# Two transformer blocks on one core: modulation rows among the natural projections, attention's left-over work in slots, overflow loops last, SyncE loads

## The chip, the core and the metric

The kernel is one program on one core of a Trainium2 chip. The metric is the device time of one execution in microseconds (us). A core has five instruction streams: TensorE (PE; its weight loads are listed as PEld), VectorE (DVE), ScalarE (ACT), GpSimd (POOL) and SyncE (SP). SP, POOL and ACT also start DMA transfers. Each stream runs its instructions in order and waits on semaphores for the others.

## What is computed

A sequence of 1024 latent rows of width 1024 (and 256 context rows) goes through two blocks. Block one modulates its normed rows by `silu(c) @ w_ada + b_ada`, runs differential attention (4 heads, two softmax maps a head) and gated linear attention (GLA), and then a mixture of 32 experts, two for each row. Block two has a gated linear recurrence, multi-head latent attention, and a mixture of 64 experts, two for each row. All is float32.

```python
shift1, scale1, gate1, shift2, scale2, gate2 = split(silu(c) @ w_ada + b_ada, 6)
h   = rms_norm(x) * (1 + scale1) + shift1
a_l = rms_norm(softmax(q0 k0) v - lam * softmax(q1 k1) v) * (1 - lambda_init)
g_l = rms_norm(gla(q, k, v, gates)) * silu(r)
x   = x + gate1 * (concat(a_l, g_l) @ w_out)
x   = x + gate2 * moe(rms_norm(x) * (1 + scale2) + shift2)     # 32 experts, top 2
x   = x + rnn_and_mla(rms_norm(x))
x   = x + moe_2(rms_norm(x))                                   # 64 experts, top 2
```

## The kernel before

The program goes through stages, one behind the other. Times are those of the profiled execution, from the start of the span:

1. **Front** (0 to about 100). The modulation that the first projection needs is made, the rows are normed, modulated and split into a high and a low half (`hTh`, `hTl`); every projection is three matmuls, high by high, low by high and high by low.
2. **Natural projections** (to about 412, loop at L395): `plan` lists slabs of 256 columns of `w_in`; `nat` does one tile of 128 rows for a slab (24 matmuls of 256 columns), and the result `po` goes to DRAM (`gqk`, `gv`, `sg`, `vs`). Between the tiles `gla_units` (L465) runs GLA step by step; it reads its values as one tile `g_v` for each of two halves `p`.
3. **Heads** (to about 541): `heads` makes the transposed queries and keys with their rotary embedding and writes them to `qs` and `ks`. Between its blocks it takes two steps of `ada_rows` (L236), which makes the four remaining parts of the modulation (gate1, shift2, scale2, gate2) as rows: a 512 KB load `wada`, two DVE multiply-adds over 128x512 into `aacc` (L250, L252), and after every fourth step a matmul `ad` that sums the partitions (L257), an addition (L258) and a store to `rows`. There are 32 steps.
4. **Attention** (to about 870): `phase1b` (L760) walks `da_units` (L662): 4 query blocks by 4 heads by 2 maps. The scores `s` of a map are copied out with their maximum (`da_e`, L697), exponentiated on ACT, and weighted on POOL or DVE. What is left (`da_turn` L722 turns the weights, `da_out` L731 multiplies by the values, norms the head with a POOL power at L745 and writes it) sits in one list `late` that keeps three items waiting. Between the maps another generator takes a step: `out_weights` (L961) first, then `mix_units` (L777) of the query block before.
5. **Mix and routing** (`phase1c`, L1002, to about 950), which also issues the first expert loads.
6. **Experts of block one** (`moe1`, L1227, to about 1515): 24 rounds of 8 MB of weights (`m_w`, loaded by SP), a gather `m_x`, and a scatter-add `x1d<-m_y` on POOL.
7. **Block two**: norms, recurrence, gates, latent attention, output (to about 2655).
8. **Experts of block two** (`moe2`, L1943, to the end): 32 pairs of experts, for each pair 6 MB of weights (`n_w`, `n_d`), a gather `n_x` and a scatter-add `out<-n_y`. SP loads the first pairs; from pair 3 on POOL issues the loads (`load(p + 3, ..., nc.gpsimd)`), behind the scatter of the pair.

`overflow` (L1085) is a loop over experts that got more rows than their capacity, with a trip count read from memory (`nc.values_load`, then `tc.For_i`, L1125 and L1126). Its count is zero here. All five streams go through the loop's branch, and POOL waits there for every transfer that it has started. It stands in round 15 of `moe1` (L1312) and behind pair 25 of `moe2` (L2037).

The order inside a stream is set by a scheduling layer that records the stages and interleaves them; the order rows below show the outcome.

Of the kernel before, what the change touches and what calls it, by code (L numbers as in the profile page):

```python
# [13 lines left out]
ALU = mybir.AluOpType  # L14
# [8 lines left out]
NA = 10  # L23
# [44 lines left out]
class Kern:  # L68
# [110 lines left out]
    def phase1a(self, keep, dram):  # L179
# [12 lines left out]
        with tc.tile_pool(name="p1a", bufs=1) as pool, tc.tile_pool(name="p1a_ps", bufs=1, space=PSUM) as psum:  # L192
# [43 lines left out]
            def ada_rows(ap):  # L236


                todo = [(s, h) for s in range(4, 12) for h in range(4)]
                ws = [ada_load(ap, *x, 3) for x in todo[0:3]]  # L240
                for n, (s, h) in enumerate(todo):
                    if h == 0:
                        acc = self.t(ap, [P, 512], tag="aacc", bufs=2)
                        row = self.t(ap, [1, 2, 512], tag="arow", bufs=2)
                        nc.sync.dma_start(row[:, 0, :], a["b_ada"][:, ts(s, 512)])
                    w = ws.pop(0)
                    for i in range(2):
                        c = c16[:, 2 * h + i:2 * h + i + 1]
                        if h + i == 0:
                            nc.vector.tensor_scalar(acc, w[:, 0, :], c, None, op0=ALU.mult)  # L250
                        else:
                            nc.vector.scalar_tensor_tensor(acc, w[:, i, :], c, acc, op0=ALU.mult, op1=ALU.add)  # L252
                    if n + 3 < len(todo):
                        ws.append(ada_load(ap, *todo[n + 3], 3))
                    if h == 3:
                        pb = self.t(psum, [P, 512], tag="ad", bufs=2)
                        self.mm(pb[0:1, :], self.mats[:, 6, 0:1], acc, True, True)  # L257
                        nc.vector.tensor_tensor(row[:, 1, :], row[:, 0, :], pb[0:1, :], op=ALU.add)  # L258
                        nc.sync.dma_start(self.rows[s // 2 - 2:s // 2 - 1, ts(s % 2, 512)], row[:, 1, :])
                    yield  # L260

# [125 lines left out]
            gla = self.gla_units(gp, psum)  # L387
            ready = {0: 2, 1: 5}
            done, waiting = 0, next(gla)
            w = slab(*first, raw)  # L390
            for i, (cols, n, tiles, fin) in enumerate(plan):
# [3 lines left out]
                for t in tiles:  # L395
                    nat(w, n, t, fin)
                    if waiting is None or i >= ready[waiting]:
                        waiting = next(gla, 2)
                        if waiting == 2:
                            ready[2] = 99  # L400
                w = nxt
            while waiting != 2:
                waiting = next(gla, 2)
            gla_cm.__exit__(None, None, None)
# [5 lines left out]
            with tc.tile_pool(name="p1a_r", bufs=1, reuse_waits="tile") as back:  # L410
                rope = self.t(back, [P, 2, S], tag="rope")
                nc.gpsimd.dma_start(rope, a["k_rope"])
                rows = ada_rows(back)
# [41 lines left out]
                for _ in rows:  # L455
                    pass
# [8 lines left out]
    def gla_units(self, pool, psum):  # L465
# [18 lines left out]
        for p in range(2):  # L484
            yield p
            v = self.t(pool, [P, NA, 256], tag="g_v")
            nc.sync.dma_start(v, self.gv[:, ts(p, 256)].rearrange("(t p) n -> p t n", p=P))
# [47 lines left out]
            def stage_b(t, qk, eb, ei, er):  # L535
# [4 lines left out]
                nc.vector.tensor_tensor(four(kt), k4, four(er if t < 2 else ei), op=ALU.mult)  # L540
                kv = [self.t(psum, [P, 256], tag="g", bufs=3) for c in range(2)]
                for h in range(2):
                    for c in range(2):
                        self.mm(kv[c][:, ts(h, P)], kt[64 * c:64 * c + 64, ts(h, P)], v[64 * c:64 * c + 64, t, ts(h, P)],
                                True, True)
# [45 lines left out]
            def stage_d(t, sm):  # L591
                s0 = P * (t - 2)
                po = self.t(psum, [P, 2, P], tag="g", bufs=3)
                for h in range(2):
                    for d in range(2):
                        self.mm(po[:, h, :], sm[:, d, h, :], v[:, t, ts(h, P)], d == 0, False)
# [48 lines left out]
    def da_load(self, qb, h):  # L645
# [12 lines left out]
        v = self.t(self.daq, [P, NA, P], tag="da_v", bufs=2)  # L658
        nc.sync.dma_start(v, self.vs[:, ts(h, P)].rearrange("(t p) n -> p t n", p=P))
        self.da_in[qb, h] = qd, kst, v  # L660

    def da_units(self, pool, psum, cp):  # L662
# [14 lines left out]
        late = []  # L677
        kb = [(0, 512), (512, 512), (1024, 256)]
        for qb in range(4):
            for h in range(4):  # L680
                qd, kst, v = self.da_in.pop((qb, h))
                if qb < 3 or h < 3:
                    self.da_load(*((qb, h + 1) if h < 3 else (qb + 1, 0)))
                groups = [self.t(pool, [P, 4, 256], tag="da_a", bufs=4) for g in range(3)]
                es0 = self.t(pool, [P, 2], tag="da_es", bufs=3)
                for j in range(2):
# [4 lines left out]
                    for m in range(2):  # L691
# [9 lines left out]
                        es.append(e)  # L701

# [19 lines left out]
    def da_turn(self, psum, e, groups, j):  # L722
        nc = self.nc
        for g in range(3):
            nk = 4 if g < 2 else 2
            pt = self.t(psum, [P, 4, P], tag="tp", bufs=3)
# [1374 lines left out]
```

## Time and profile before

| | |
|---|---|
| median of 3 runs | 3222.18 us (3221.11 to 3223.78) |
| profiled execution | 3225.12 us, of which its span is 3223.3 us |
| busy in the span | PE 90%, DVE 42%, ACT 31%, POOL 15% |
| mean granted TensorE clock | 0.958 of full speed |
| moved by DMA | 705.72 MB, mean 219 GB/s |

Busy shares are means over stages with different limits, so the profile is read stage by stage: in the table of windows below, an engine near the length of its window is what bounds that window. The last two columns are the share of time in which the 16 DMA engines were busy, and the bytes that they moved. The groups of rows further below are numbered for the text that follows them.

### The profile page before, as it was taken

The page shows a single profiled execution, that of the slowest core. Times are in us where ns is not written, and L with a number is a line of the kernel's source. Part 1 is how long each engine was busy: PE and PEld are TensorE (multiplying, and loading weights), DVE is VectorE, ACT ScalarE, POOL GpSimd, SP SyncE. Part 2 cuts the span into 40 slices and gives each one's busy share as a digit, 9 for nine tenths or more (in the row PEclk, how much of TensorE's full clock was granted, in tenths as well). Part 3 has the DMA queues.
Part 4 walks back from the last instruction along what each step waited for, and adds up shares of the span by engine and source line. Part 5 has one row for each costly group of instructions (what it writes and reads, how often), then busy time and mean ns, then how long its engine had stood idle before and what let it go on. Part 6 is the DMA issues. An engine that isn't in the chain of part 4 may idle for free.

```text
span 3223.3 us, 45952 instructions
## 1 busy us (share of the span) xinstructions
PE 2895.1 (90%) x17841; PEld 1945.5 (60%) x17841; DVE 1365.4 (42%) x3217; ACT 985.8 (31%) x2006; POOL 482.3 (15%) x520
## 2 busy tenths in 40 slices
PE   6999997799969999897899999999998988777758
PEld 4989875677743333232777788878876973323223
DVE  4244377867651111111567512478875361111101
ACT  4355311555410000000656413256664111100001
POOL 2000011222210101000100000111001103333332
PEclk8999998899989999999899999999999999999989
DMA  6223278676478999995422443322246469999988
GB/s 220 92 83 102 82 249 233 172 182 171 136 298 332 391 403 400 345 393 205 156 65 82 137 161 113 108 74 66 56 121 209 149 233 364 407 378 365 394 330 299
DMA packets 282109, 705.72 MB, mean 219 GB/s; under 512 B 33784, under 2 KB 168080, under 8 KB 233120
## 3 DMA queue, kind: packets, MB, share of 16 engines
q1 hardware_dynamic: 230880, 462.06, 42.4%
q0 software_dynamic: 44320, 222.85, 18.9%
q10 hardware_dynamic: 6688, 17.83, 1.5%
q8 instruction: 142, 2.33, 0.3%
q14 instruction: 79, 0.65, 0.1%
HBM read 616.08 MB, written 99.11 MB: 222 GB/s over the span
## 4 chain that ended last, share of the span: by engine, by line
PE 24%; DMA 17%; DVE 6%; ACT 2%; issue 2%; POOL 1%; SPq 0%; POOLq 0%; DVEq 0%; ACTq 0%
PE mm L88 19%; DMA n_d<-exp_w 12%; DMA n_w<-exp_w 2%; PE s L88 1%; PE o L88 1%; PE gt L88 1%; DMA oTs<-od 1%; POOL m_rs L101 1%; DMA ws<-w_mla_o 1%; DVE wl L1340 1%; PE tp L1868 1%; PE lg L88 0%; DVE m_al L1872 0%; ACT wh L1339 0%; DVE m_e L1847 0%
## 5 line engine op out<-in xcount | busy, mean ns | idle before, releaser
L88 PE MATMUL mm<-m_w,m_xTf 128*32 128x512 f32 x3072 | 343.4, 599 | 10.0 <-issue 10.0
L88 PE MATMUL mm<-n_w,n_xTf 128*64 128x512 f32 x1024 | 268.2, 637 | 83.9 <-DMA n_w<-exp_w 62.7
L88 PEld LDWEIGHTS mm<-n_w,n_xTf 128*64 128x64 f32 x1024 | 91.1, 147 | 254.9 <-issue 254.3
L88 PEld LDWEIGHTS mm<-m_w,m_xTf 128*32 128x32 f32 x3072 | 96.0, 111 | 221.2 <-issue 215.3
L88 PE MATMUL mm<-uTh,wh 128*128 128x512 f32 x512 | 205.4, 401 | 0.0
L88 PE MATMUL mm<-uTh,wl 128*128 128x512 f32 x512 | 203.4, 397 | 0.0
L88 PE MATMUL mm<-uTl,wh 128*128 128x512 f32 x512 | 202.5, 396 | 0.0
L88 PE MATMUL mm<-wh,hTh 128*128 128x256 f32 (+1 forms) x608 | 178.1, 293 | 1.9 <-ACT wh L288 1.9
L88 PE MATMUL mm<-wh,hTl 128*128 128x256 f32 (+1 forms) x608 | 176.0, 289 | 1.7 <-DVE hTl L351 1.7
L88 PE MATMUL mm<-wl,hTh 128*128 128x256 f32 (+1 forms) x608 | 175.0, 288 | 0.5 <-DVE wl L289 0.5
L88 PE MATMUL mm<-m_w,m_hTf 128*32 128x512 f32 x1536 | 171.1, 592 | 0.9 <-DVE m_hTf L1071 0.9
L1340 DVE TENSOR_TENSOR wl<-ws,wh 128x512 fp32r<-128x512 f32 x128 | 90.0, 717 | 167.7 <-ACT wh L1339 167.4
L1071 ACT COPY m_xTf<-tp 128x512 f32<-128x512 f32 x24 | 14.1, 586 | 426.5 <-PE tp L1065 392.3
L2023 DVE TENSOR_TENSOR n_h<-n_h,mm 128x256 f32<-128x256 f32 x32 | 13.5, 421 | 306.4 <-ACT n_h L2022 306.4
L88 PE MATMUL s<-da_k,da_q 128*128 128x512 f32 (+1 forms) x384 | 117.4, 414 | 14.9 <-DVE da_e L697 14.5
L88 PE MATMUL mm<-n_d,n_hTf 128*64 128x512 f32 x512 | 117.0, 598 | 14.1 <-DVE n_hTf L1071 14.0
L1287 DVE SCALAR_TENSOR_TENSOR m_y<-mm,o_w,gt 128x512 f32<-128x512 f32 x48 | 36.0, 751 | 213.7 <-PE mm L88 210.8
L88 PEld LDWEIGHTS mm<-wh,hTh 128*128 128x128 f32 x608 | 115.9, 191 | 9.8 <-issue 5.6
L88 PEld LDWEIGHTS mm<-m_w,m_hTf 128*32 128x32 f32 x1536 | 50.4, 110 | 115.9 <-issue 115.2
L88 PEld LDWEIGHTS mm<-wh,hTl 128*128 128x128 f32 x608 | 116.0, 191 | 4.1 <-DVE hTl L351 2.7
L88 PEld LDWEIGHTS mm<-wl,hTh 128*128 128x128 f32 x608 | 116.1, 191 | 2.9 <-issue 1.3
L1339 ACT CAST wh<-ws 128x512 fp32r<-128x512 f32 x128 | 77.6, 619 | 128.7 <-PE mm L88 51.2
(542 smaller groups left out, 6533.2 us busy)
## 6 DMA issues: line engine op xcount, KB each, us to landing
n_w<-exp_w POOLq DMA_DIRECT2D x112, 1024.0 KB, 17.0
m_w<-expert_w_gate SPq DMA_DIRECT2D x64, 1024.0 KB, 10.0
m_w<-expert_w_up SPq DMA_DIRECT2D x64, 1024.0 KB, 10.5
m_w<-expert_w_down SPq DMA_DIRECT2D x64, 1024.0 KB, 13.5
n_d<-exp_w POOLq DMA_DIRECT2D x58, 1024.0 KB, 16.8
wada<-w_ada SPq DMA_DIRECT2D x48, 512.0 KB, 4.8
da_k<-ks SPq DMA_DIRECT2D x64, 320.0 KB, 6.3
n_w<-exp_w SPq DMA_DIRECT2D x12, 1024.0 KB, 8.6
```

The costliest lines, as they stand in the source:

```text
L88: self.nc.tensor.matmul(out, l, r, start=start, stop=stop)
L101: nc.gpsimd.tensor_tensor(out, m, self.neghalf[:, 0:w], op=ALU.pow)
L1071: (nc.scalar.copy if g else nc.vector.tensor_copy)(xf[:, r, :], pt)
L1287: nc.vector.scalar_tensor_tensor(y[:, ts(c, 512)], py[c], rt["w"][:, r:r + 1], gt2[:, ts(c, 512)], op0=ALU.mult, op1=ALU.mult)
L1339: nc.scalar.copy(wh[:, r, :], st)
L1340: nc.vector.tensor_tensor(wl[:, r, :], st, wh[:, r, :].bitcast(F32), op=ALU.subtract)
L1868: nc.tensor.transpose(pt[:, i, :], e[:, ts(g0 + i, P)], self.ident)
L2023: nc.vector.tensor_tensor(h, h, ph[:, 1, :], op=ALU.mult)
```

## The change

It has seven parts.

- **Rows.** `ada_rows` works in 128 steps: a 128 KB load `wrow`, one DVE multiply-add over 128x256. There are 16 matmuls `ad` of 256 columns, each done six steps after its sum is complete. Two steps stand behind each tile of the natural projections from the second slab on.
- **GLA values.** Instead of one `g_v` tile for each half, each step loads its own 128x256 tile, once for the states and once for the output: 36 loads of 128 KB in place of 2 of 1280 KB.
- **Attention.** Each head yields four times, and the left-over work of the head before stands in four slots: turn, turn, product with the values, sum of squares; the norm follows one slot later. `phase1b` takes a step of the other generator in three of the four. The value load `da_v` moves to the start of its head.
- **Mix.** `mix_units` yields once more in each half; `phase1c` issues its 8 first expert loads one at a time.
- **Loop of `moe1`** behind the last round. **Loop of `moe2`** behind the last pair.
- **Loads of `moe2`** are all issued by SP.

```diff
...
+                todo = [(s, k) for s in range(8, 24) for k in range(8)]
+                def load(s, k):
+                    w = self.t(ap, [P, 256], tag="wrow", bufs=3)
+                    nc.sync.dma_start(w, wa[:, k, ts(s, 256)])
...
+                def finish(s, acc, row):
+                    pb = self.t(psum, [P, 512], tag="ad", bufs=2)
+                    self.mm(pb[0:1, 0:256], self.mats[:, 6, 0:1], acc, True, True)
+                    nc.vector.tensor_tensor(row, row, pb[0:1, 0:256], op=ALU.add)
+                    nc.sync.dma_start(self.rows[s // 4 - 2:s // 4 - 1, ts(s % 4, 256)], row)
...
+                ws, late = [load(*x) for x in todo[0:2]], None
+                for n, (s, k) in enumerate(todo):
+                    w, c = ws.pop(0), c16[:, k:k + 1]
+                    if k == 0:
+                        acc = self.t(ap, [P, 256], tag="aacc", bufs=2)
+                        row = self.t(ap, [1, 256], tag="arow", bufs=2)
+                        nc.sync.dma_start(row, a["b_ada"][:, ts(s, 256)])
+                        nc.vector.tensor_scalar(acc, w, c, None, op0=ALU.mult)
+                    else:
+                        nc.vector.scalar_tensor_tensor(acc, w, c, acc, op0=ALU.mult, op1=ALU.add)
+                    if n + 2 < len(todo):
+                        ws.append(load(*todo[n + 2]))
+                    if k == 5 and late:
+                        finish(*late)
+                    if k == 7:
+                        late = s, acc, row
                     yield
+                yield
+                yield
+                finish(*late)
...
                     nat(w, n, t, fin)
+                    if i:
+                        next(rows, None)
+                        next(rows, None)
...
-                            if c0 >= 256:
-                                next(rows, None)
-                                next(rows, None)
...
-            v = self.t(pool, [P, NA, 256], tag="g_v")
-            nc.sync.dma_start(v, self.gv[:, ts(p, 256)].rearrange("(t p) n -> p t n", p=P))
+            def values(t, tag):
+                v = self.t(pool, [P, 256], tag=tag, bufs=2)
+                nc.sync.dma_start(v, self.gv[ts(t, P), ts(p, 256)])
...
+                v = values(t, "g_v1")
...
-        v = self.t(self.daq, [P, NA, P], tag="da_v", bufs=2)
-        nc.sync.dma_start(v, self.vs[:, ts(h, P)].rearrange("(t p) n -> p t n", p=P))
-        self.da_in[qb, h] = qd, kst, v
+        self.da_in[qb, h] = qd, kst
...
+        behind = [[], [], [], []]
...
+        def slot(i):
+            while behind[i]:
+                f, x = behind[i].pop(0)
+                f(*x)
...
-                    late.append((self.da_turn, (psum, es[0], groups, j)))
-                    if j == 1:
-                        late.append((self.da_out, (pool, psum, cp, h, qb, v, groups, es0)))
-                    while len(late) > 3:
-                        f, x = late.pop(0)
-                        f(*x)
-                    yield qb
-        for f, x in late:
-            f(*x)
...
+                    mine.append((pool, psum, es[0], groups, j))
+                    slot(2 * j + 1)
+                    yield qb, 2 * j + 1
+                state = {}
+                behind[0].append((self.da_turn, mine[0]))
+                behind[1].append((self.da_turn, mine[1]))
+                behind[2].append((self.da_out, (pool, psum, v, groups, state)))
+                behind[3].append((self.da_ssq, (pool, psum, es0, state)))
+                behind[3].append((behind[0].append, ((self.da_norm, (psum, cp, h, qb, state)),)))
+        for i in (0, 1, 2, 3, 0):
+            slot(i)
+            yield qb, -1
...
+    def da_ssq(self, pool, psum, es0, state):
...
+    def da_norm(self, psum, cp, h, qb, state):
...
-            for i, qb in enumerate(self.da_units(pool, psum, cp)):
-                if qb != at and i % 8 >= 2:
+            for i, (qb, slot) in enumerate(self.da_units(pool, psum, cp)):
+                if qb != at and i % 16 >= 4:
                     for _ in other:
                         pass
                     other, at = self.mix_units(cp, psum, lg, qb - 1, 1, 3), qb
-                if i:
+                if i and slot != 2:
                     next(other, None)
...
+                    if k == 3:
+                        yield
...
-                if i < 4:
-                    self.moe1_load()
+                if i < 8:
                     self.moe1_load()
...
-                if r == 15:
-                    self.overflow(pool, psum, "m_", rt, self.h2d, self.x1d, wg.rearrange("e d h -> (e d) h"),
-                                  wu.rearrange("e d h -> (e d) h"), wd.rearrange("e h d -> (e h) d"), E, HID, self.cap1, gt2)
             down(ROUNDS - 1, self.turn_cols(pool, psum, h, 4, "m_hT", False))
+            self.overflow(pool, psum, "m_", rt, self.h2d, self.x1d, wg.rearrange("e d h -> (e d) h"),
+                          wu.rearrange("e d h -> (e d) h"), wd.rearrange("e h d -> (e h) d"), E, HID, self.cap1, gt2)
...
-                        eng.dma_start(w[i][:, j, k, :], m[es[i]].rearrange("(p k) n -> p k n", k=8)[:, k, :])
+                        nc.sync.dma_start(w[i][:, j, k, :], m[es[i]].rearrange("(p k) n -> p k n", k=8)[:, k, :])
...
-                    if p == 25:
-                        self.overflow(pool, psum, "n_", rt, self.h4d, self.x3d, wg.rearrange("e d h -> (e d) h"),
-                                      wu.rearrange("e d h -> (e d) h"), wd.rearrange("e h d -> (e h) d"), E, HID, cap)
                     if p + 3 < E // 2:
-                        load(p + 3, 2 if p + 4 == E // 2 else 1, nc.gpsimd)
+                        load(p + 3, 2 if p + 4 == E // 2 else 1)
+                self.overflow(pool, psum, "n_", rt, self.h4d, self.x3d, wg.rearrange("e d h -> (e d) h"),
+                              wu.rearrange("e d h -> (e d) h"), wd.rearrange("e h d -> (e h) d"), E, HID, cap)
...
```

Three places in the order of the program. First, PE at the end of `heads` and the first scores of attention (`mm` are the projections, `ad` sums a modulation row, `s` are the scores). Before:

```order
L88 MATMUL mm_5443<-hTl_109,wh_5033 128x512
L88 MATMUL ad_5363<-aacc_5308,mats_75 1x512
L88 MATMUL mm_5443<-hTh_108,wl_5034 128x512
...
L88 MATMUL mm_5443<-hTh_108,wl_5034 128x512
L88 MATMUL ad_5483<-aacc_5434,mats_75 1x512
L88 MATMUL s_5537<-da_k_5228,da_q_5227 128x512 x2
```

The changed kernel:

```order
L88 MATMUL mm_5829<-hTl_109,wh_5499 128x512
L88 MATMUL mm_5829<-hTh_108,wl_5500 128x512
L88 MATMUL s_5912<-da_k_5648,da_q_5647 128x512 x2
L88 MATMUL s_5916<-da_k_5648,da_q_5647 128x512 x2
L88 MATMUL s_5920<-da_k_5648,da_q_5647 128x256 x2
```

The last `ad` stood between the last projection and the first scores; now the scores follow the projections directly, and the 16 `ad` matmuls stand among the natural projections.

Second, SP in the second half of the natural projections of the changed kernel, where before only stores of `po` (`vs`, `sg`), GLA's transfers and the slab loads `wst` stood:

```order
L501 DMA g_v_825_3967<-gv_64 128x256
L289 DMA wst_5105<-w_in 128x4x256
L518 DMA g_qk_4030<-gqk_63 128x256
L376 DMA vs_62<-po_3931 128x256
L251 DMA rows_67<-arow_3386 1x256
L244 DMA wrow_4117<-w_ada 128x256
L244 DMA wrow_4175<-w_ada 128x256
L376 DMA vs_62<-po_4021 128x256
L244 DMA wrow_4178<-w_ada 128x256
L259 DMA arow_4111<-b_ada 1x256
L501 DMA g_v_843_4053<-gv_64 128x256
```

SP's queue now holds 128 `wrow` loads and 36 `g_v` loads between stores that wait for their `po`.

Third, POOL and SP around the two loops (the rows of L1125, L1126, L1168 and L1169 are the loop; `m_w`, `n_w` and `n_d` are weights). POOL in `moe2` before:

```order
L1081 DMA out<-n_y_25261,o_tok_21276 1024x1024
L1967 DMA n_w_4304_23582<-exp_w_2 128x2048
L1125 TENSOR_LOAD v_ni_25292
L1126 COMPARE_AND_BRANCH
L1126 ISA
...
L1967 DMA n_w_4304_23582<-exp_w_2 128x2048
L1970 DMA n_d_4306_23584<-exp_w_2 128x2048
```

POOL in `moe2` of the changed kernel:

```order
L1124 DMA out<-n_y_25894,o_tok_21656 1024x1024
L1124 DMA out<-n_y_25948,o_tok_21656 1024x1024
L1124 DMA out<-n_y_25989,o_tok_21656 1024x1024
L1168 TENSOR_LOAD v_ni_26020
L1169 COMPARE_AND_BRANCH
L1169 ISA
```

SP at the end of `moe1` of the changed kernel, where `norm_g` is the first load of block two:

```order
L1268 DMA m_w_2538_12867<-expert_w_down 128x2048
L1168 TENSOR_LOAD v_ni_13066
L1168 ISA x2
L1169 COMPARE_AND_BRANCH
...
L1543 DMA g_2667_13448<-norm_g 128x1024
L1379 DMA wzs_2670_13452<-w_in 128x4x288
```

The loop of `moe2` stood between two weight loads of POOL and now stands behind the last scatter, with no weight load left on POOL. The loop of `moe1` stands behind the last weight load and ahead of block two's first loads.

## Rows read from the trace of the kernel before

**Rows 1.** The page, busy time of the engines.
```profile
PE 2895.1 (90%) x17841; PEld 1945.5 (60%) x17841; DVE 1365.4 (42%) x3217; ACT 985.8 (31%) x2006; POOL 482.3 (15%) x520
```

**Rows 2.** Windows: natural, heads, its end, attention (two), moe1 (two), moe2's stop.
```profile
core 0: us, PE busy (x) PEld busy (x) DVE busy (x) ACT busy (x) POOL busy (x), PEclk, DMA share, GB/s
100.00:412.00 312.00, 311.93 (x2450) 279.90 (x2449) 122.88 (x343) 151.34 (x476) 11.73 (x17) 1.00 0.32 96
412.00:530.00 118.00, 107.80 (x472) 81.29 (x470) 95.17 (x149) 14.81 (x23) 21.01 (x15) 0.96 0.79 251
530.00:541.00 11.00, 2.05 (x3) 0.35 (x4) 7.50 (x15) 1.24 (x2) 1.26 (x1) 0.55 0.73 219
541.00:641.00 100.00, 77.12 (x330) 61.54 (x331) 84.04 (x218) 52.81 (x81) 23.26 (x9) 0.81 0.71 181
641.00:870.00 229.00, 223.30 (x1199) 181.54 (x1199) 156.63 (x463) 121.10 (x204) 54.50 (x32) 0.99 0.66 167
1000.00:1300.00 300.00, 300.00 (x2692) 100.13 (x2688) 45.33 (x65) 15.39 (x26) 34.13 (x26) 1.00 1.01 397
...
3100.00:3112.00 12.00, 5.63 (x29) 2.69 (x29) 2.20 (x4) 1.66 (x3) 2.66 (x5) 0.98 1.02 399
3112.00:3136.00 24.00, 2.76 (x12) 1.74 (x12) 0.69 (x1) 0.59 (x1) 3.68 (x4) 0.50 0.48 185
3136.00:3160.00 24.00, 22.64 (x102) 8.22 (x102) 3.83 (x7) 2.04 (x4) 9.26 (x14) 0.94 0.81 295
```

**Rows 3.** Timeline of POOL around moe1's loop (start, duration, engine, line, idle before).
```profile
1282.92 1.59 POOL L1081 DMA_INDIRECT x1d<-m_y,o_tok  x1 [19.50 <-DVE m_y L1287]
...
1305.56 1.58 POOL L1081 DMA_INDIRECT x1d<-m_y,o_tok  x1 [19.69 <-DVE m_y L1287]
...
1315.93 1.03 POOL L1075 DMA_INDIRECT m_x<-h2d,o_tok  x1 [7.42 <-PEq L1126]
1342.73 1.62 POOL L1081 DMA_INDIRECT x1d<-m_y,o_tok  x1 [25.77 <-DMA m_w<-expert_w_gate]
```

**Rows 4.** Timeline of PE and SP at moe1's loop.
```profile
1305.78 1.10 SPq L1225 DMA_DIRECT2D m_w<-expert_w_gate  x1
...
1325.29 0.33 SPq L1225 DMA_DIRECT2D m_w<-expert_w_up  x1
...
1325.67 4.79 PE L88 MATMUL mm<-m_w,m_xTf 128*32 128x512 f32 x24 [10.02 <-issue]
```

**Rows 5.** Timeline at the end of moe1: last scatter, then SP's next load.
```profile
1516.40 1.56 POOL L1081 DMA_INDIRECT x1d<-m_y,o_tok  x1 [14.87 <-DVE m_y L1287]
1522.85 0.33 SPq L1500 DMA_DIRECT2D g<-norm_g  x1
```

**Rows 6.** Windows: DMA share at the end of moe1's loads.
```profile
1490.00:1500.00 10.00, 10.00 (x100) 3.01 (x96) 1.50 (x2) 0.00 (x0) 0.03 (x1) 1.00 0.01 2
```

**Rows 7.** Timeline of POOL and PE at moe2's loop.
```profile
3115.72 0.58 POOL L1967 DMA_DIRECT2D n_w<-exp_w  x1 [0.43 <-issue]
3135.61 0.55 POOL L1967 DMA_DIRECT2D n_w<-exp_w  x1 [19.30 <-DVE n_xTf L1071]
...
3134.87 9.03 PE L88 MATMUL mm<-n_w,n_xTf 128*64 128x512 f32 x32 [21.24 <-issue]
```

**Rows 8.** DMA queues (packets, MB, share): moe1 1000:1300, two rows; then moe2 2800:3100.
```profile
q1 hardware_dynamic: 15053, 109.60, 88.8%
q0 software_dynamic: 3744, 9.09, 11.5%
...
q0 software_dynamic: 19412, 114.91, 99.8%
```

**Rows 9.** Groups by line, 412:541: DVE sums and the PE matmul behind them.
```profile
L252 DVE SCALAR_TENSOR_TENSOR aacc<-wada,c,aacc 128x512 f32<-128x512 f32 x56 | 49.8, 890 | 2.0 <-DMA wada<-w_ada 1.6
L88 PE MATMUL ad<-aacc,mats 128*1 128x512 f32 x16 | 9.8, 701 | 19.1 <-DVE aacc L252 19.1
```

**Rows 10.** Timeline of PE at the border of heads and attention.
```profile
538.95 1.86 PE L88 MATMUL ad<-aacc,mats 128*1 128x512 f32 x2 [10.96 <-DVE aacc L252]
540.74 1.65 PE L88 MATMUL s<-da_k,da_q 128*128 128x512 f32 x3
```

**Rows 11.** Waits of PE in attention, 541:870 (total, times, longest).
```profile
PE s L88 <- DVE da_e L697: 14.5, 10, 3.7
PE tp L88 <- POOL da_rs L745: 9.5, 12, 1.5
```

**Rows 12.** Natural projections: landing of 128 KB loads; waits of SP, first row.
```profile
g_qk<-gqk SPq DMA_DIRECT2D x20, 128.0 KB, 2.0
...
SPq L364 <- ACT po L363: 85.3, 44, 8.2
```

More of the change, by code (lines that the diff above doesn't have):

```diff
@@ L236, in ada_rows @@
             def ada_rows(ap):
[L239 to L259, printed above, removed]
@@ L387, in phase1a @@
             gla = self.gla_units(gp, psum)
+            rows = ada_rows(np_)
             ready = {0: 2, 1: 5}
@@ L403, in phase1a @@
                 waiting = next(gla, 2)
+            for _ in rows:
+                pass
             gla_cm.__exit__(None, None, None)
@@ L412, in phase1a @@
                 nc.gpsimd.dma_start(rope, a["k_rope"])
-                rows = ada_rows(back)
                 swap = [(i + 16) % 32 for i in range(32)]
@@ L454, in phase1a @@
                     w = nxt
-                for _ in rows:
-                    pass
         self.dump("d_qs", self.qs)
@@ L540, in stage_b @@
                 nc.vector.tensor_tensor(four(kt), k4, four(er if t < 2 else ei), op=ALU.mult)
+                v = values(t, "g_v0")
                 kv = [self.t(psum, [P, 256], tag="g", bufs=3) for c in range(2)]
@@ L676, in da_units @@
         nc.vector.tensor_scalar(nlam, nlam, -self.lambda_init, None, op0=ALU.add)
-        late = []
+        behind = [[], [], [], []]
         kb = [(0, 512), (512, 512), (1024, 256)]
+        def slot(i):
+            while behind[i]:
+                f, x = behind[i].pop(0)
+                f(*x)
         for qb in range(4):
             for h in range(4):
-                qd, kst, v = self.da_in.pop((qb, h))
+                qd, kst = self.da_in.pop((qb, h))
+                v = self.t(self.daq, [P, NA, P], tag="da_v", bufs=2)
+                nc.sync.dma_start(v, self.vs[:, ts(h, P)].rearrange("(t p) n -> p t n", p=P))
                 if qb < 3 or h < 3:
                     self.da_load(*((qb, h + 1) if h < 3 else (qb + 1, 0)))
-                groups = [self.t(pool, [P, 4, 256], tag="da_a", bufs=4) for g in range(3)]
+                groups = []
                 es0 = self.t(pool, [P, 2], tag="da_es", bufs=3)
+                mine = []
                 for j in range(2):
@@ L701, in da_units @@
                         es.append(e)
+                        if m == 0:
+                            slot(2 * j)
+                            yield qb, 2 * j
                     rr = self.t(pool, [P, 1], tag="da_rr", bufs=3)
@@ L725, in da_turn @@
             nk = 4 if g < 2 else 2
+            if j == 0:
+                groups.append(self.t(pool, [P, 4, 256], tag="da_a", bufs=4))
             pt = self.t(psum, [P, 4, P], tag="tp", bufs=3)
@@ L729, in da_turn, with da_out @@
             (nc.vector.tensor_copy if g == 0 else nc.scalar.copy)(groups[g][:, 0:nk, ts(j, P)], pt[:, 0:nk, :])
-    def da_out(self, pool, psum, cp, h, qb, v, groups, es0):
+    def da_out(self, pool, psum, v, groups, state):
         nc = self.nc
@@ L735, in da_out @@
             self.mm(po, v[:, kt, :], groups[kt // 4][:, kt % 4, :], kt == 0, kt == NA - 1)
-        oT = self.t(pool, [P, 256], tag="da_o", bufs=2)
+        oT = state["o"] = self.t(pool, [P, 256], tag="da_o", bufs=2)
         nc.scalar.copy(oT, po)
-        sq = self.t(pool, [P, 256], tag="da_sq", bufs=1)
+        sq = state["sq"] = self.t(pool, [P, 256], tag="da_sq", bufs=1)
         nc.scalar.activation(sq, oT, AF.Square)
+    def da_ssq(self, pool, psum, es0, state):
+        nc = self.nc
         pn = self.t(psum, [P, 256], tag="tp", bufs=3)
         for j in range(2):
-            self.mm(pn[:, j:j + 1], sq[:, ts(j, P)], self.mats[:, 6, 0:1], True, True)
-        rs = self.t(pool, [P, 2], tag="da_rs", bufs=2)
+            self.mm(pn[:, j:j + 1], state["sq"][:, ts(j, P)], self.mats[:, 6, 0:1], True, True)
+        rs = state["rs"] = self.t(pool, [P, 2], tag="da_rs", bufs=2)
         nc.vector.scalar_tensor_tensor(rs, pn[:, 0:2], 1.0 / 128, es0, op0=ALU.mult, op1=ALU.add)
         nc.gpsimd.tensor_tensor(rs, rs, self.neghalf[:, 0:2], op=ALU.pow)
+    def da_norm(self, psum, cp, h, qb, state):
+        nc = self.nc
+        rs, oT = state["rs"], state["o"]
         pn = self.t(psum, [P, 256], tag="tp", bufs=3)
@@ L1956, in moe2, with load @@
                     dt[i] = self.t(wp, [P, 2, D], tag="n_" + n)
-            def load(p, halves=1, eng=nc.sync):
+            def load(p, halves=1):
                 es = p, p + E // 2
```

10 lines of the change are left out of this document (6 added, 4 removed).

## Prediction

> **What bounds the kernel now.** I read the page's busy times first, then the table of windows, then in each stage that the change touches the timeline, the waits and the DMA queues. The page says that TensorE (PE) is busy for 90% of the span [rows 1], which hides that stages differ. The windows show it [rows 2]. In the natural projections PE is busy for 311.93 of 312 us at full clock: whatever is added to PE there is paid in full, whatever is added to another engine may be free. In the heads PE is busy for 107.80 of 118 us, DVE for 95.17, and 49.8 us of DVE's time are the sums `aacc` [rows 9]. Then PE stands almost still for 11 us. In the first 100 us of attention PE is busy for 77.12 us at a clock of 0.81, DVE for 84.04; in the rest PE is busy for 223.30 of 229 us. `moe1` is PE's again, 300 of 300 us, but the DMA engines are as busy (1.01). In `moe2` the DMA engines bound (1.02 at 3100) while PE has idle time, up to the stop at 3112.
>
> The sum is made against the profiled execution (3225.1 us), 2.9 us above the median of 3222.2 us. I carry the difference over to the median. 0.2% (6.4 us) is about what a measurement can tell from no change.
>
> **The natural projections get more work.** The `ad` matmuls sum as many columns as before (16 of 256 for 8 of 512). Before they took 9.8 us, the last 1.86 of them at a low clock [rows 9, 10]; I take +9 us here, since PE has no gap (between 0, if they overlap their neighbours, and 9.8). DVE gets 128 operations of half the old width. At half of 890 ns [rows 9] that is 57 us, on top of 122.88 us of 312 [rows 2]: not a bound. The `wrow` loads move 16.8 MB where the DMA engines are busy for 0.32. SP also issues 36 `g_v` loads. A 128 KB load lands in 2.0 us [rows 12], and a load that is issued ahead costs PE nothing. I take 0 because most of a tile's 24 matmuls can lie between issue and use. The other end is each of them waited for: 36 x 2.0 = 72 us.
>
> **Heads.** The window of 118 us holds 107.80 us of PE work, of which `ad` is 9.8 - 1.86 = 7.9 us [rows 2, 9]. What stays is 99.9 us. Of the 10.2 us of idle time I leave half, for the embedding's chain through POOL and ACT that opens the stage. Attention's first scores would then start at 412 + 99.9 + 5 = 517 instead of 540.74 [rows 10], for in the new order they follow the last projection directly and no longer stand behind an `ad` that waited 10.96 us for DVE. **-23.8 us**, between -28.8 (no idle time left) and -18.6 (all of it left).
>
> **Attention.** PE waits here for two things of note: 14.5 us for DVE to copy scores out, 9.5 us for the POOL power behind the sum of squares, 12 times [rows 11]. The new slots put the norm one slot behind that power, so I take the 9.5 us as gone. The wait for DVE stays: `out_weights` gives DVE the same work before the next query block. The bounds are 0 (PE meets DVE's queue sooner) and the idle time that even DVE's 84.04 us would allow: 16 in the first 100 us and 5.7 in the rest, 21.7 [rows 2]. **-9.5 us.** What is late next is DVE's copy of the scores. The added yields of `mix_units` and the eight single expert loads issue the same work; the loads lie beside routing, so I cost them at nothing. If that cover were gone, one late load of 1.05 MB would cost 2.7 us (2.54 us a MB, worked out below from [rows 8]).
>
> **The loop in `moe1`.** Scatters come every 1305.56 - 1282.92 = 22.64 us, but 37.17 us across the loop [rows 3], so it costs 14.5 us: PE has no instruction for 10.02 us, and SP issues no load from 1305.78 to 1325.29 [rows 4]. This goes. At the new place the branch costs again. There POOL must see its last transfer land, then let the others go. Mid-stage, 8.3 us passed between the end of POOL's last issue (1315.93 + 1.03) and SP's next load; at the end of `moe1`, without a loop, SP already waits 4.9 us from the end of the scatter's issue (1517.96) to 1522.85 [rows 3 to 5]. The difference, 3.4 us, is the price of the loop at a border (between 0 and the full 14.5). **-14.5 + 3.4 = -11.1 us.**
>
> **The loop in `moe2`.** POOL stood for 19.30 us, PE for 21.24 us [rows 7]. What counts here is DMA time, as the stage is bound by it: against 1.02 before, 24 us at 0.48 and 24 us at 0.81 lose 12.7 + 4.9 = 17.6 us [rows 2]. By the bytes (185 and 295 against 399 GB/s) it is 19.2 us. I take 17.6, and 3.4 us for the loop behind the last scatter: **-14.2 us**.
>
> **Loads of `moe2` on SP.** POOL's loads stood behind its scatter; SP's do not, but the DMA engines were full all the same (0.998 of 300 us, [rows 8]), so an earlier issue gains nothing. The queue itself may be faster. With SP's loads, `moe1` needed 1.003 x 300 / 118.69 = 2.54 us for a MB; with POOL's, `moe2` needed 0.998 x 300 / 114.91 = 2.61 us [rows 8]. Over 29 pairs of 6.3 MB that would be 13 us. I take 0, since the two stages mix loads, gathers and scatters differently, and keep -13 as the other end (and nothing on the side of a loss: at 1.0 the engines can't be made busier).
> The Trainium skill (DMA: Bandwidth & Descriptors, "Issuing engines are not separate DMA queues") says that transfers of all issuers share the same 16 engines and that another issuer only saves issue time. By that rule the term is 0 and the sum stays at 3173 us; by the two rows it would be 3160 us.
>
> **The sum.** +9 - 23.8 - 9.5 - 11.1 - 14.2 = -49.6 us, that is 3175.5 us for the profiled execution and **3173 us** for the median.
>
> **The rivals.**
> - **Late values (slower).** SP runs in order, and its queue among the tiles waits for `po` in 44 places, 85.3 us in all [rows 12]. A `g_v` load behind such a store starts only when the tile is done, and the GLA matmul that needs it holds PE, which is the bound. Up to 36 x 2.0 = 72 us: 3245 us. It decides from 49.6 / 36 = 1.4 us a load on. For it: the `g_v` rows stand right among these stores. Against it: GLA's existing loads (`g_qk`) go through the same queue, and PE is at 311.93 of 312.
> - **Less in heads and attention.** DVE or the embedding's chain takes the place of what goes: heads -18.6, attention 0, together 14.7 us less: 3188 us. For it: DVE's 84.04 us of 100 in the first query block; against it: PE waited 14.5 us for DVE's copies in all of attention [rows 11], so DVE was seldom far behind.
> - **The faster queue**, as above: 3160 us. Against it: the engines are shared.
> - **Loads set `moe1`'s pace.** In 300 us SP's queue brought 109.60 MB, 13.07 rounds of 8.39 MB, while PE used 300 / 22.64 = 13.25 [rows 3, 8]. If the lead ran out, a round would take 22.95 us, 24 of them 7 us more: 3180 us. Against it: after the stop the loads were still done by 1490 (0.01 busy, [rows 6]), 26 us ahead of the last scatter.
> The Trainium skill (DMA: Bandwidth & Descriptors, Specifications) gives about 358 GB/s of memory bandwidth for a core, by which the loads would set the pace already; the trace's 397 GB/s [rows 2] disagrees, and the measurement decides.
>
> **How the numbers follow.** Forecast 0.58; less in heads and attention 0.17; faster queue 0.10; loads' pace 0.05; late values 0.10, of which 0.07 reach beyond no change and 0.03 land within it. So faster 0.90, same 0.03, slower 0.07. The range is 3148 (the faster queue, and attention at its bound of 21.7 us) to 3203 (less in heads and attention, and 15 us of late values, 0.42 us a load).
>
> **What would show it.** Right: scores start near 517 plus the 9 us of the natural stage (526); scatters of `moe1` 22.6 us apart throughout; no dip of DMA in `moe2`; POOL's waits for `da_rs` gone from PE. Wrong: idle time of PE before GLA's matmuls in the natural stage, waiting for `g_v`; PE waiting for `m_w`; a stop of more than 4 us behind the last scatter of `moe1`; a DMA share under 1.0 in the middle of `moe2`.

## The result, and the profile after

The changed kernel takes **3170.4 us** (median of 4 runs, 3166.64 to 3174.28). The kernel before, run beside it on the same chip, takes 3221.64 us. The ratio is 0.984, with an interval of 0.9827 to 0.9853. So the gain is 51.2 us where 49.6 were forecast, and the time lies inside the range. The parts of the sum fared less well than the sum.

The profiled execution of the changed kernel is its fastest (3166.64 us, span 3164.8), and that of the kernel before its slowest (3225.12 us). The spans differ by 58.5 us, and I cut them at the same instructions on both sides:

| stretch, and what marks its ends | forecast | measured |
|---|---|---|
| natural projections, to the first 512-column `mm` of the heads (406.70, now 415.79) | +9 | +9.1 |
| heads, to the first score `s` (540.74, now 516.05) | -23.8 | -33.8 |
| attention, mix and routing, to the first `m_xTf` matmul (953.8, now 907.5) | -9.5 | -21.6 |
| `moe1`, to its last scatter (1516.40, now 1475.74) | -14.5 | **+5.6** |
| from there to the first `a_rs` of block two (the moved loop) | +3.4 | +2.9 |
| to the first gather of `moe2` (2657.11, now 2611.34; the change doesn't touch it) | 0 | -8.1 |
| `moe2`, to its last scatter (3216.69, now 3154.33) | -17.6 | -16.6 |
| from there to the end of the span (the moved loop) | +3.4 | +3.9 |

The -8.1 is not the change's. From the last scatter of `moe1` to the first gather of `moe2` the kernel before took 1140.7 us in this profile, but four kernels below that alter nothing in between (`attn_only`, `rows_only`, `loop2_end`, `sp_loads`) took 1132.3 to 1134.7. The profile of before carries it. The difference of the medians, 51.2 us, is smaller than that of the spans by about as much.

The page of the changed kernel, its first part (to be held against [rows 1]):

```profile
PE 2895.8 (91%) x17857; PEld 1945.5 (61%) x17857; DVE 1374.1 (43%) x3289; ACT 988.2 (31%) x2006; POOL 379.7 (12%) x342
```

The windows of the changed kernel: natural, heads, attention (first 100 us and part of the rest), `moe1`, the end of `moe2`. The columns are those of [rows 2].

```profile
100.00:412.00 312.00, 310.59 (x2427) 273.15 (x2427) 173.08 (x468) 149.65 (x472) 11.90 (x16) 1.00 0.48 142
416.00:516.00 100.00, 100.00 (x480) 82.97 (x480) 50.61 (x87) 16.10 (x25) 20.35 (x16) 1.00 0.51 163
516.00:616.00 100.00, 80.40 (x384) 62.34 (x384) 87.78 (x236) 59.10 (x91) 20.18 (x10) 0.86 0.84 213
616.00:870.00 254.00, 247.79 (x1353) 205.07 (x1352) 183.93 (x547) 125.85 (x216) 61.29 (x41) 0.99 0.62 169
1190.00:1450.00 260.00, 260.00 (x2170) 88.21 (x2166) 36.55 (x52) 12.43 (x21) 24.29 (x19) 1.00 0.93 359
3100.00:3112.00 12.00, 9.15 (x42) 3.62 (x40) 2.29 (x4) 1.66 (x3) 1.56 (x1) 0.98 1.01 417
3112.00:3136.00 24.00, 21.41 (x90) 8.23 (x88) 3.14 (x6) 2.04 (x4) 1.55 (x1) 0.94 0.88 293
3136.00:3160.00 24.00, 14.49 (x66) 4.55 (x64) 2.35 (x4) 1.76 (x3) 3.10 (x2) 0.92 0.29 76
```

PE stays full in the natural projections beside DVE's added work, is busy for all of the 100 us of the heads, and has no stop in `moe2`. One row looks harmless and isn't. In `moe1`, 1190 to 1450, PE is busy for 260.00 of 260 us at full clock, as before. But it did 2170 matmuls, 8.35 a us, where before it did 2692 in 300 us, 8.97 a us [rows 2]. A full PE did 7% less work.

The scatters show since when. Timeline of POOL in `moe1` of the changed kernel (as [rows 3]):

```profile
1235.91 1.58 POOL L1124 DMA_INDIRECT x1d<-m_y,o_tok  x1 [19.50 <-DVE m_y L1330]
1258.55 1.57 POOL L1124 DMA_INDIRECT x1d<-m_y,o_tok  x1 [19.70 <-DVE m_y L1330]
1287.05 1.61 POOL L1124 DMA_INDIRECT x1d<-m_y,o_tok  x1 [8.52 <-DVE m_y L1330]
1308.48 1.58 POOL L1124 DMA_INDIRECT x1d<-m_y,o_tok  x1 [19.82 <-DVE m_y L1330]
1333.23 1.58 POOL L1124 DMA_INDIRECT x1d<-m_y,o_tok  x1 [21.81 <-DVE m_y L1330]
...
1475.74 1.55 POOL L1124 DMA_INDIRECT x1d<-m_y,o_tok  x1 [16.58 <-DVEq L1169]
```

Up to 1258.55 the scatters are 22.64 us apart, then 28.50, 21.43 and 24.75, and that triple repeats: 74.68 us for three rounds in place of 67.9. From the first scatter to the last it is 536.2 us, where before, stop included, it was 529.9.

### The profile page after: what moved, and what is told of

Read it like the earlier page. It is cut to its first block, busy times and chain, and to the rows that moved or that the text cites. A ratio compares the mean times of both kernels' runs of the same rounds, so it can differ in the third digit from the quotient of the medians.

```text
span 3164.8 us, 46430 instructions
## 1 busy us (share of the span) xinstructions
PE 2895.8 (91%) x17857; PEld 1945.5 (61%) x17857; DVE 1374.1 (43%) x3289; ACT 988.2 (31%) x2006; POOL 379.7 (12%) x342
## 5 line engine op out<-in xcount | busy, mean ns | idle before, releaser
L88 PE MATMUL mm<-m_w,m_xTf 128*32 128x512 f32 x3072 | 364.3, 595 | 0.0
L88 PE MATMUL mm<-n_w,n_xTf 128*64 128x512 f32 x1024 | 277.9, 645 | 61.9 <-DMA n_w<-exp_w 61.8
L88 PEld LDWEIGHTS mm<-m_w,m_xTf 128*32 128x32 f32 x3072 | 103.6, 110 | 214.5 <-issue 208.3
L88 PE MATMUL mm<-m_w,m_hTf 128*32 128x512 f32 x1536 | 190.1, 598 | 0.9 <-DVE m_hTf L1114 0.9
L88 PE MATMUL s<-da_k,da_q 128*128 128x512 f32 (+1 forms) x384 | 105.6, 397 | 14.0 <-DVE da_e L724 11.3
```

The costliest lines, as they stand in the source:

```text
L88: self.nc.tensor.matmul(out, l, r, start=start, stop=stop)
```

## Where the time of `moe1` went

My first theory was order. The scheduling layer moves matmuls of neighbouring blocks past one another. The loop in the middle was a cut that nothing could pass. Without it, the layer mixes gate and up (`m_xTf`), down (`m_hTf`) and the transposes on PE. The rival was loads: SP's loads no longer keep up once the stop is gone (the rival "loads set `moe1`'s pace" of the prediction).

The timeline of PE in the changed kernel, in the third of those rounds:

```profile
1308.38 10.51 PE L88 MATMUL mm<-m_w,m_xTf 128*32 128x512 f32 x96
1318.82 0.75 PE L1108 MATMUL tp<-mats,m_h 128*128 128x128 f32 x4
1319.50 1.06 PE L88 MATMUL mm<-m_w,m_xTf 128*32 128x512 f32 x6
1320.38 0.59 PE L88 MATMUL mm<-m_w,m_hTf 128*32 128x512 f32 x1
1320.39 0.62 PE L88 MATMUL mm<-m_w,m_xTf 128*32 128x512 f32 x1
1320.81 0.59 PE L88 MATMUL mm<-m_w,m_hTf 128*32 128x512 f32 x1
1320.84 0.59 PE L88 MATMUL mm<-m_w,m_xTf 128*32 128x512 f32 x1
1321.24 0.59 PE L88 MATMUL mm<-m_w,m_hTf 128*32 128x512 f32 x1
1321.25 0.63 PE L88 MATMUL mm<-m_w,m_xTf 128*32 128x512 f32 x3
```

The first row is the regular order. 96 matmuls of 0.59 us each are done in 10.51 us, 0.11 us apart, so several run at once. Each uses 32 of the array's columns (128*32). The Trainium skill (TensorE: Matmul & The Clock Gate, "Part 3: Packing small matmuls — row/col tiling") says that small matmuls that lie on distinct column groups run concurrently, and the row agrees. In the mixed rows one `m_hTf` and one `m_xTf` start together, and the next two follow 0.43 us later: two matmuls in the time that four took. No row shows idle time, since one matmul or another is always in flight.

The waits of the changed kernel, 1190 to 1480, on SP and on PE:

```profile
SPq L1268 <- PE mm L88: 196.5, 44, 14.9
```

```profile
PE mm L88 <- DVE m_hTf L1114: 0.9, 1, 0.9
PE tp L1108 <- DVE m_h L1354: 0.9, 1, 0.9
```

The loads wait for PE, 196.5 us in all. PE never waits for a load. That speaks against the rival before any run.

## The experiments

**1. The loop back in the middle of `moe1`**, everything else as changed.

```diff
+                if r == 15:
+                    self.overflow(pool, psum, "m_", rt, self.h2d, self.x1d, ...)
             down(ROUNDS - 1, self.turn_cols(pool, psum, h, 4, "m_hT", False))
-            self.overflow(pool, psum, "m_", rt, self.h2d, self.x1d, ...)
```

> The changed kernel with moe1's loop put back into round 15; all else as changed. Order theory (without the loop the schedule of moe1 mixes the projection's and the down matmuls from the 17th round on, which costs 20 us, more than the loop's 14.5 us): the 24 rounds shorten from 568 to 563 us, the border behind them by another 3 us, so 3161 to 3163 us. Loads theory (the rounds are slow because the weights come late once the stop is gone): the stop comes on top of the slow rounds, 3177 to 3185 us. Border theory (only the loop's price at the border was mis-sized): 3175 us or more.

Measured: 3164.35 us, ratio 0.9828 (0.9811 to 0.9844). It is not slower than the changed kernel. The intervals overlap, so a gain isn't shown by the medians. From first to last scatter it needs 531.6 us, the stop included, against 536.2: the stop costs less than what its removal brought with it.

**2. Matmul blocks pinned.** Each gate, up and down block of `moe1` must be issued after the last matmul recorded before it. Nothing else changes.

```diff
-        self.nc.tensor.matmul(out, l, r, start=start, stop=stop)
+        self.last = self.nc.tensor.matmul(out, l, r, start=start, stop=stop).ins
...
+            def pin(f, r, *x):
+                if not r:
+                    return f(r, *x)
+                with tc.issue_after(self.last):
+                    f(r, *x)
...
-                gate_up(r, 0, ph)
+                pin(gate_up, r, 0, ph)
```

> The changed kernel, with each block of moe1's matmuls (four quarters of gate and up, and the down product) told to be issued behind the block before it on TensorE; same instructions. Order theory: the rounds go back to 22.6 us throughout, 20 us off the 568, so about 3150 us. Loads theory: PE now waits openly for m_w, the rounds stay at 24.9 us and the time at 3170 us. In between, if a part of the slow rounds was late weights: 3155 to 3165 us with waits of PE for m_w in the trace.

Measured: 3153.7 us, ratio 0.9799 (0.9783 to 0.9816), clear of the changed kernel's interval. The triple shrinks to 25.86, 21.46 and 22.63 us, 69.95 for three rounds, and no matmul of PE waits for a load in them. Not all of the loss is gone, since the transposes of the next round's input still move.

**3. The loop of `moe1` at the end, alone**, in the kernel before.

```diff
-                if r == 15:
-                    self.overflow(pool, psum, "m_", rt, self.h2d, self.x1d, ...)
             down(ROUNDS - 1, self.turn_cols(pool, psum, h, 4, "m_hT", False))
+            self.overflow(pool, psum, "m_", rt, self.h2d, self.x1d, ...)
```

> The kernel before with moe1's loop alone moved behind the last round. Order theory: 6 us more in the rounds and 3 us more at the border, 3230 us. Prediction as it was on record (14.5 us for the stop, 3.4 us for the border): 3210 us.

Measured: 3224.21 us against 3218.94 beside it, ratio 1.0017 (1.0008 to 1.0027). The edit that I costed at -11.1 us makes the kernel slower when done by itself: 534.5 us from first to last scatter in place of 529.9. So neither the loads moved to SP nor the earlier start has a part in it.

**4. The attention slots alone** (slots, the added yields, the single loads), in the kernel before; of its diff the core:

```diff
-        late = []
+        behind = [[], [], [], []]
...
+                        if m == 0:
+                            slot(2 * j)
+                            yield qb, 2 * j
...
+                behind[3].append((self.da_ssq, (pool, psum, es0, state)))
+                behind[3].append((behind[0].append, ((self.da_norm, (psum, cp, h, qb, state)),)))
```

> The kernel before with the attention slots alone (left-over work in four slots, value load at the head's start, three steps of the other generator a head, the added yield and the eight single expert loads); modulation rows stay in the heads, loops and loads stay. In the changed kernel attention and routing took 391 us where they had taken 413. Slots theory (the 21.6 us come from the slots): 3200 to 3205 us. DVE theory (they come from the sums that no longer fill DVE's queue at the border, the slots themselves give about the 9.5 us of the POOL waits or less): 3212 to 3222 us.

Measured: 3199.19 us, ratio 0.9936 (0.992 to 0.9953). From the first score (here at 539.66) to `moe1`'s first matmul (933.31) it needs 393.65 us, 19.4 less than before. That is most of the -21.6 of the changed kernel, and twice my term. Its waits, 541 to 870, against [rows 11]:

```profile
PE s L88 <- DVE da_e L706: 9.6, 9, 2.8
PE tp L745 <- DVE da_nm L708: 3.4, 4, 2.7
...
PE tp L88 <- POOL da_rs L765: 2.0, 4, 1.1
```

The windows of the kernel before and of this one, from the first score to `moe1`'s first matmul, then the first 120 us of it in either:

```profile
540.74:953.80 413.06, 353.39 (x1798) 283.43 (x1798) 289.77 (x866) 186.68 (x316) 93.98 (x59) 0.92 0.67 187
540.74:660.74 120.00, 96.43 (x439) 77.72 (x439) 100.01 (x264) 64.40 (x101) 26.87 (x11) 0.83 0.71 180
```

```profile
539.66:933.31 393.65, 344.01 (x1799) 279.37 (x1799) 291.25 (x866) 187.42 (x316) 88.91 (x59) 0.92 0.69 196
539.66:659.66 120.00, 101.64 (x480) 80.35 (x480) 100.31 (x267) 66.56 (x103) 21.80 (x11) 0.88 0.79 201
```

PE's idle time falls from 59.7 to 49.6 us. The larger part is what I took: the wait for `da_rs` went from 9.5 to 2.0 us. The wait for DVE's `da_e`, which I had left as it was, fell too, from 14.5 to 9.6, and a new one for `da_nm` gives 3.4 of that back. The other 9.4 us are *busy* time: the same matmuls keep PE busy for less. The 256 long score matmuls go from 92.8 to 86.6 us, for example. Two things lie in that. The granted clock comes back sooner (0.89 and 1.00 in 581:621 and 621:661, where before it was 0.84 and 0.89). Over the first 120 us it is 0.88 in place of 0.83, and 0.95 in both behind them; 0.05 of 120 us is 6 us, which I take as an estimate of its part. And work that no longer has a wait between its parts overlaps. I didn't run them apart.

**5. The rows and the values alone** (modulation among the natural projections, single `g_v` loads), in the kernel before; of its diff the core:

```diff
-                rows = ada_rows(back)
...
+            rows = ada_rows(np_)
...
+                    if i:
+                        next(rows, None)
+                        next(rows, None)
...
+                v = values(t, "g_v0")
```

> The kernel before with the modulation rows among the natural projections and the GLA values loaded tile by tile; attention, loops and moe2's loads as before. Additive theory: the first scores come 24.7 us earlier, as in the changed kernel, and nothing else moves: 3193 to 3198 us. Rival (a part of attention's gain comes from here, since DVE enters attention without a backlog): 3185 us or less. Late-values theory: 3210 us or more, with PE idle ahead of GLA's matmuls.

Measured: 3197.28 us, ratio 0.9926 (0.991 to 0.9943), 25.0 us less than beside it, for two terms that made -14.8 in my sum. The profile has no wait of PE in the heads any more, and `s` follows the last projection directly. From the first score to `moe1`'s first matmul this kernel needs 412.7 us (before 413.1), so attention's gain doesn't come from here. Timeline of PE in the changed kernel, as [rows 10]:

```profile
515.82 0.40 PE L88 MATMUL mm<-hTh,wl 128*128 128x512 f32 x1
516.05 0.62 PE L88 MATMUL s<-da_k,da_q 128*128 128x512 f32 x2
```

**6. The loop of `moe2` at the end, alone**, the loads left on POOL.

```diff
-                    if p == 25:
-                        self.overflow(pool, psum, "n_", rt, self.h4d, self.x3d, ...)
                     if p + 3 < E // 2:
                         load(p + 3, 2 if p + 4 == E // 2 else 1, nc.gpsimd)
+                self.overflow(pool, psum, "n_", rt, self.h4d, self.x3d, ...)
```

> The kernel before with moe2's loop alone behind the last pair; POOL still issues the loads. Stop theory: the DMA time of the stop comes back (17.6 us) and the loop costs 3.9 us at the end, 3204 to 3207 us. Queue theory (the gain in moe2 is SP's queue, the stop is made up by the DMA engines anyway): 3215 us or more.

Measured: 3212.4 us, ratio 0.9971 (0.9962 to 0.9981). Within `moe2` 547.6 us in place of 559.6, so -12.0, and then 12.5 us from the last scatter to the end in place of 6.6. That lies between the two theories: the stop's time comes back, but not all of it. PE's rows behind the old place of the stop show why, first of the kernel before, then of this one:

```profile
3149.37 7.04 PE L88 MATMUL mm<-n_w,n_xTf 128*64 128x512 f32 x32
3161.88 7.04 PE L88 MATMUL mm<-n_w,n_xTf 128*64 128x512 f32 x32
```

```profile
3134.91 7.05 PE L88 MATMUL mm<-n_w,n_xTf 128*64 128x512 f32 x30 [2.59 <-DMA n_w<-exp_w]
3151.63 7.05 PE L88 MATMUL mm<-n_w,n_xTf 128*64 128x512 f32 x30 [2.61 <-DMA n_w<-exp_w]
```

Behind the stop the pairs came 12.5 us apart, and PE waited for no load in them. Without it they come 16.7 us apart, with a wait for a load in each. So the kernel before made up a part of the stop behind it.

**7. The loads of `moe2` on SP, alone**, the loop left at pair 25.

```diff
-                        load(p + 3, 2 if p + 4 == E // 2 else 1, nc.gpsimd)
+                        load(p + 3, 2 if p + 4 == E // 2 else 1)
```

> The kernel before with moe2's weight loads on SP alone; the loop stays behind pair 25, where SP now waits too. Shared engines theory: no change, 3216 to 3222 us, the loads at 2.6 us a MB. Queue theory: up to 13 us faster, 3206 us.

Measured: 3210.29 us, ratio 0.9967 (0.9958 to 0.9977), although the stop is still there and longer. Timeline of POOL, then of PE, around it:

```profile
3094.09 1.61 POOL L1081 DMA_INDIRECT out<-n_y,o_tok  x1 [0.30 <-issue]
3132.37 1.57 POOL L1081 DMA_INDIRECT out<-n_y,o_tok  x1 [36.66 <-DVE n_y L2035]
```

```profile
3116.36 8.70 PE L88 MATMUL mm<-n_w,n_xTf 128*64 128x512 f32 x32 [23.84 <-issue]
```

The gain lies ahead of the stop. From the first gather to the scatter of pair 25 it needs 446.1 us, before 456.5. The DMA queues in 2800:3090 (packets, MB, share of the engines), of `loop2_end` with POOL's loads, then of `sp_loads`:

```profile
DMA packets 18781, 111.20 MB, mean 383 GB/s; under 512 B 4239, under 2 KB 4239, under 8 KB 6196
...
q0 software_dynamic: 18769, 111.04, 99.7%
```

```profile
DMA packets 19224, 113.35 MB, mean 391 GB/s; under 512 B 4408, under 2 KB 4408, under 8 KB 6389
...
q1 hardware_dynamic: 14425, 105.04, 89.7%
q0 software_dynamic: 4786, 8.13, 11.0%
```

With the engines full in both, the same stage moves 2% more bytes a second. It does so in every kernel here: in 2800:3080, 382 to 384 GB/s in the five whose `moe2` loads through POOL, 390 to 392 in the five that load through SP. From the first gather to the scatter of pair 25 the five with POOL's loads need 454.3 to 456.5 us, the five with SP's 446.1 to 450.1. The Trainium skill (DMA: Bandwidth & Descriptors, "Issuing engines are not separate DMA queues") says that another issuer only saves issue time. These runs don't agree, and the measurement decides. A single packet is not faster: those of 8 KB took 325 ns in the mean in `loop2_end` and 324 in `sp_loads` (2800:3080), but 12077 of them were moved in the one and 12330 in the other. What in the queue brings them closer together wasn't tried.

The two edits of `moe2` share their gain. The loop's removal is worth 12.0 us with POOL's loads, but 6.2 beside SP's (549.2 to 543.0). At the end of the changed kernel PE's last wait for a load is over at 3110.82, and in the 24 us from 3112 on PE is busy for 21.41 while the DMA share falls to 0.88: the last pairs are PE's.

**8. The transposes pinned too**, beside the blocks of run 2.

```diff
-                front(r + 1)
+                if r + 1 < ROUNDS:
+                    pin(front, r + 1)
```

> As the kernel with moe1's blocks in order, and the transposes of the next round's rows also told to follow the down product, so that no transpose stands in its middle (that cost 2.0 us in three rounds). Order theory: all rounds at 22.64 us, 23 x 22.64 less the short last one, 515 us in place of 522.7 us from first to last scatter: 3146 us. Loads theory: the rounds that were slower had hidden that the weights come at 13.07 rounds in 300 us; PE waits for m_w and 3 us or less are gained, 3151 to 3154 us.

Measured: **3147.64 us** (3144.02 to 3149.5), ratio 0.9766 (0.975 to 0.9782). It beats both kernels. From the first scatter to the last it needs 516.3 us. Timeline of PE, one round:

```profile
1259.24 10.51 PE L88 MATMUL mm<-m_w,m_xTf 128*32 128x512 f32 x96
1269.68 0.75 PE L1108 MATMUL tp<-mats,m_h 128*128 128x128 f32 x4
1270.36 3.64 PE L88 MATMUL mm<-m_w,m_xTf 128*32 128x512 f32 x32
1273.82 7.07 PE L88 MATMUL mm<-m_w,m_hTf 128*32 128x512 f32 x64
1280.82 1.16 PE L1108 MATMUL tp<-mats,m_x 128*128 128x128 f32 x8
```

The same work, unmixed. In three rounds of the changed kernel 192 `m_hTf` matmuls keep PE busy for 27.5 us; here they do for 21.2 (the groups by line):

```profile
L88 PE MATMUL mm<-m_w,m_hTf 128*32 128x512 f32 x192 | 27.5, 594 | 0.0
```

```profile
L88 PE MATMUL mm<-m_w,m_hTf 128*32 128x512 f32 x192 | 21.2, 592 | 0.0
```

One of them takes the same 0.59 us in both; only the overlap differs. And with the order restored the loads keep up without the stop (1.01 DMA share and 397 GB/s in 1000:1300, as before), so the loads' pace falls as a rival.

## Why the prediction was right, and where it wasn't

**The sum** came out 2.6 us above the measured median because errors cancel: heads and attention gave 22 us more than forecast, `moe1` 20 us less, and `moe2` came out right for a partly wrong reason. That the sum is so close is luck.

**Natural projections (+9): right.** PE has no gap there, so the `ad` matmuls were paid in full. The late values, my slower rival, did not come: PE was busy for 310.59 of 312 us, and 36 loads ahead of use cost nothing that shows.

**Heads (-23.8, measured -33.8): mis-sized, by a reading.** The step that failed is "of the 10.2 us of idle time I leave half, for the embedding's chain". The group row of `ad` had the answer: 19.1 us of idle time, all of it ended by DVE's `aacc` [rows 9]. All idle time of PE in the heads was the sums'. None was left once they were gone. That is 5 us more. The window of the whole heads of the kernel before gives the rest:

```profile
407.00:541.00 134.00, 114.85 (x497) 85.70 (x496) 104.69 (x165) 17.30 (x27) 22.88 (x17) 0.92 0.78 245
```

Without the `ad` matmuls that is 114.85 - 9.8 = 105 us of PE for the projections. Now they take 100.3 us, at a granted clock of 1.00. Before, the clock was 0.92 over the whole window, and 0.96 ahead of the last stop [rows 2]; 0.04 of those 118 us is 4.7 us, about the difference. It was lowest in 424:436 (0.72), where PE waited 3.97 us for a sum. I had carried their length over as it was. The waits had also cost clock.

**Attention (-9.5, measured -21.6; alone -19.4): mis-sized.** The step "I take the 9.5 us as gone" held for 7.5 of them: `da_rs` went from 9.5 to 2.0. "The wait for DVE stays" did not hold: it fell by 4.9 us. In all PE's idle time fell by 10, about the size of my term. What I left out is that PE's busy time isn't fixed. It held matmuls at a reduced clock and without overlap behind the waits, 9.4 us of them.

**The loop of `moe1` (-11.1, alone +5.3): wrong in sign.** The price of the stop was right: with the order pinned, the stage from first to last scatter loses 13.6 us (529.9 to 516.3) where I had 14.5. Three things make up the 13.6. The stop cost 13.3 us, since the scatter behind it followed after 21.43 us, 1.2 less than a regular round. The kernel before had also lost 2.0 us ahead of its 13th and 14th scatter (26.20 and 21.12 us) to transposes inside the down product, which the pins end. And the last round of run 8 is 1.7 us longer than that of the kernel before (18.13 us to 16.43), for a reason that stays open. The price at the border was right too, 2.9 against 3.4. SP's next load comes 7.6 us after the scatter's issue, before 4.9. What failed is the step "This goes", which takes the rounds on both sides of the stop as given. They were regular because a loop stood between them. I named loads as what could eat the gain, and it was the order of PE's own queue. The rows of the order on which the prediction rests are those of POOL and SP at the loops; PE's in the rounds behind the old place are not among them.

**`moe2` (-14.2, measured -12.7): right in sum, by two terms.** I had the loop at -17.6 and the loads on SP at 0. Alone, within the stage, they are -12.0 and -10.4, together -16.6. The rival "faster queue" was right on the loads: its two rows of [rows 8] (2.54 and 2.61 us a MB) showed what five kernels against five confirm. I set it aside since "the engines are shared". They are, and its 13 us came as 10.4 where the stop was kept. The step that failed on the loop is "What counts here is DMA time": it took the 17.6 us of lost DMA time as lost up to the end. But behind the stop the pairs ran at PE's pace, 12.5 us each, and 12.0 us were lost.

**Still open.** Why the layer begins to mix only after 16 rounds was not tested. The two kernels without a loop in the middle and without pins (the changed one, run 3) show it; the kernel before and run 1 do not. Nor was it tried what makes SP's loads 2% faster, or how much of attention's shorter busy time is the clock and how much overlap.

## What to carry to other kernels

When an instruction that stops all engines is moved out of a loop, read the order of the bounding engine behind its old place, not only the stop: it may have kept a scheduler from mixing work, and its removal may need a pin in its stead. An engine at 100% busy and full clock can still slow down, so divide the number of its instructions by the window before calling it unchanged. And before idle time is shared out among causes, look at the group's own "idle before" column, which names the one that ended it.

## What the runs showed of the hardware

Matmuls that use 32 of the array's columns run 0.11 us apart in a regular order. When matmuls of two accumulations alternate singly, pairs of them start 0.43 us apart. One matmul lasts 0.59 us in both cases, with no idle time and no lower clock to show it. And with the loads on SP's queue the DMA engines moved 390 to 392 GB/s (2800:3080, five kernels) in a stage where with POOL's they moved 382 to 384 (five kernels), at a DMA share of 1.0 in both.
